# RWKV products by head, a compact state updated by VectorE, and the order of work around the triangular inverse

## The chip, the core and the metric

The kernel runs on one NeuronCore of a Trainium2 chip. TensorE (PE) multiplies matrices, its weight loads (PEld) running beside the products; VectorE (DVE), ScalarE (ACT) and GpSimd (POOL) work on tiles; SyncE (SP) issues most transfers. The metric is the device time of one execution in microseconds (us). Lower is better.

## The reference, cut to what matters

Two layers run over 256 context tokens and 1024 image tokens. In each a projection feeds four mixers (RWKV-7, S5, SSD, GLA), whose outputs are joined and projected back. The change touches the RWKV mixer alone: four heads, two directions, a 64x64 state S for each.

```python
def rwkv7_scan(r, w, k, v, kk, a, s0, reverse, need_out):
    def step(S, inp):
        r_t, w_t, k_t, v_t, kk_t, a_t = inp
        sa = jnp.einsum('bhvk,bhk->bhv', S, -kk_t)
        S = S * w_t[:, :, None, :] + sa[..., None] * (kk_t * a_t)[:, :, None, :] + v_t[..., None] * k_t[:, :, None, :]
        y = jnp.einsum('bhvk,bhk->bhv', S, r_t) if need_out else None
        return S, y
```

## The kernel before, in words

A layer has three stages: the projection with the GLA and SSD mixers in its shadow, the RWKV stage with the S5 mixer in its shadow, and the output projection.

The RWKV stage, `rw`, walks ten windows of 128 tokens, both directions at once. A window has two chunks `s` of 64 tokens. The index `u`, 0 to 3, is direction times two plus head pair. A head pair fills 128 partitions, head `h` in its 64-partition half. Five steps stand one iteration apart, so that iteration `i` holds step `st` of window `i - st`:

- `rw_elem` (0): decays and scaled keys: `AR` (the operands that meet the state), `BK`, the chunk decay `PM`, the bonus sum `ks`.
- `rw_pair` (1): the products of `BK` and `AR` within a chunk, masked into `A`. As both heads lie under one another, `AR` is first copied by POOL into a zeroed tile `r_AD` that keeps the heads apart. `BK`, scaled and transposed, becomes `Bt`; 32x32 diagonal blocks of `A` are copied to `r_Ad` by ACT.
- `rw_inv` and `rw_vals` (2): the inverse of the triangular matrix, `TT`. VectorE transposes `r_Ad` into `r_N`, then does fifteen dependent pairs `r_tp`, `r_X`, then transposes and four small products.
- `rw_chain` (3): the only serial work between windows, twice per window: products with `UV` and `S` into `X`, a copy to `rs`, the product with `TT`, a copy into `UV`, the product with `Bt`, the new `S`. The outputs gather in the same bank as `X` and leave it as `yw`.
- `rw_out` and `rw_final` (4): outputs are moved out of `yw` by products with the constant `IJ`, summed over directions in `r_yt`, normed and gated.

The state `S`, `rs` and `TT` hold both heads on the diagonal of a zeroed [128, 4, 128] (or [128, 8, 64]) tile. A product with a bf16 zero tile `r_z` opens each `X` bank.

The Tile framework draws dependences and waits. A list scheduler sets each engine's order: among what is ready by its own model it takes what was traced first. `ORDER = (3, 2, 4, 1, 0)` is the order of tracing within an iteration; S5 quarters, `gelu` and `gate` (`side`, at iterations `SJ`) are traced ahead of it. Each engine then runs its own list strictly in order.

Of the kernel before, what the change touches and what calls it, by code (L numbers as in the profile page):

```python
# [15 lines left out]
OP = mybir.AluOpType  # L16
# [71 lines left out]
CON, ACON, RCON = {}, {}, {}  # L88
for _d, _l in ((CON, [("ident", 128), ("ones", 128), ("bones", 128), ("eps", 1), ("gneps", 1), ("one", 1)]),
               (ACON, [("triF", 128), ("triB", 128), ("gmF", 64), ("gmB", 64), ("bm4", 4), ("c16", 16), ("reset64", 256)]),  # L90
               (RCON, [("IJ", 128), ("vinit", 256), ("rm", 128), ("m16", 32), ("reset64", 256)])):
    _o = 0
    for _n, _c in _l:
        _d[_n] = (_o, _c)
        _o += _c
# [6 lines left out]
def constants():  # L102
# [24 lines left out]
    ij = np.zeros((128, 128))  # L127
    ij[64:, :64] = np.eye(64)
    ij[:64, 64:] = np.eye(64)[::-1]
    put("IJ", ij)  # L130
# [108 lines left out]
RA = "pvpv"  # L239
AA = "ppvv"  # L240

EG = dict(bk="aa", ad="pppp", dg="aaaa", bb="pp", b0="p", b1="v", tk="pp", am="p", ar="vp", sp="p", bt="aa")

RN = (3, 2, 10)
NF = 2
# [9 lines left out]
class K:  # L255
# [864 lines left out]
    def rw(self, outs, side={}):  # L1120

        nc, c = self.nc, self.c
        self.rz = {}
        for p, ns in (("re", "in th a cs eP BK AD Ad N X Am tp Rm Bb"), ("rx", "AR A"), ("rl", "ks yt fin f0 yw")):
# [9 lines left out]
        self.zero = self.S("r_z", [128, 512], mybir.dt.bfloat16)  # L1134
        nc.gpsimd.memset(self.zero, 0.0)
        self.rsc = dict(okb=okb, kah=kah, w0=w0h, a0=a0h)
        self.ks, self.yt = {}, {}
        S = None
        Ws = [dict(w=w, bi=[w, 1 - w if w < 2 else 11 - w], need=outs or w >= 2) for w in range(10)]
        for i in range(10 + 4):  # L1140
            for f in side.get(i, ()):
                f()
            for st in ORDER:
                k = i - st
                if not 0 <= k < 10:
                    continue
                W = Ws[k]
                if st == 0:
                    self.rw_elem(W)
                elif st == 1:  # L1150
                    self.rw_pair(W)
                elif st == 2:
                    self.rw_inv(W)
                    self.rw_vals(W)
                elif st == 3:
                    S = self.rw_chain(W, S)
                else:
                    self.rw_out(W)
                    if W["need"] and not self.rw_first(W, 0):
                        self.rw_final(W["bi"])  # L1160

    def rw_first(self, W, d):

# [67 lines left out]
    def rw_pair(self, W):  # L1231
# [5 lines left out]
        for d in range(2):  # L1237
            z = self.rzero("r_AD", [128, 2, 2, 2, 2, 64], 1)
            for h in range(2):
                q = slice(64 * h, 64 * h + 64)  # L1240
                self.copy(EG["ad"][2 * d + h], z[q, :, :, h, :n // 64], AR[q, d, :, :, :n // 64])
            for s in range(2):
                ps = self.P("pb")
                for hp in range(2):
                    self.mm(ps[:, hp * 256:(hp + 1) * 256], BK[:, d * 2 + hp, s].rearrange("p k t -> p (k t)"),
                            z[:, hp, s].rearrange("p h k t -> p (h k t)"))
                self.tt(A[:, s, 2 * d:2 * d + 2].rearrange("p u h f -> p (u h) f"), ps.rearrange("p (a f) -> p a f", a=4),
                        c("rm").unsqueeze(1).to_broadcast([128, 4, 128]), OP.mult)
# [21 lines left out]
    def rw_inv(self, W):  # L1270
# [11 lines left out]
        for i in range(15, 0, -1):  # L1282
            r0 = i // 4
            sh = [128, 2, i, 4 - r0]
            self.tt(tmp[:, :, :i, r0:], N[:, :, i, 0:i].unsqueeze(3).to_broadcast(sh), X[:, :, i:i + 1, r0:4].to_broadcast(sh), OP.mult)
            self.tt(X[:, :, :i, r0:4], X[:, :, :i, r0:4], tmp[:, :, :i, r0:], OP.add)
# [61 lines left out]
    def rw_chain(self, W, S):  # L1348
        nc = self.nc
        A, AR, Bt, TT, UV, PM = [W[n] for n in ("A", "AR", "Bt", "TT", "UV", "PM")]  # L1350
        w, need = W["w"], W["need"]
        if need:
            yw = W["yw"] = self.R("r_yw", [128, 2, 256], 1)
        hs = [slice(64 * h, 64 * h + 64) for h in range(2)]
        for s in range(2):
            last = w == 9 and s == 1
            X = self.P("px").rearrange("p (u f) -> p u f", u=4)
            self.mm(X.rearrange("p u f -> p (u f)"), self.zero[:, 0:128], self.zero, True, False)
            for u in range(4):
                for h in range(2):  # L1360
                    self.mm(X[0:64, u, hs[h]], A[:, s, u, h, 0:64], UV[:, s, u, hs[h]], False, False)
            if S is not None:
                for u in range(4):
                    ar = AR[:, u // 2, u % 2, s]
                    if need:
                        self.mm(X[:, u], ar.rearrange("p k t -> p (k t)"), S[:, u], False, False)
                    else:
                        self.mm(X[0:64, u], ar[:, 0], S[:, u], False, u == 3)
            rs = self.rzero("r_rs", [128, 4, 128], 2)
            nc.vector.tensor_copy(rs[0:64, :, 0:64], X[0:64, :, 0:64])  # L1370
            nc.scalar.copy(rs[64:128, :, 64:128], X[0:64, :, 64:128])  # L1371
            ps = self.P("pu")[0:64].rearrange("p (u v) -> p u v", u=4)
            for u in range(4):
                self.mm(ps[:, u], TT[:, s * 4 + u], rs[:, u])
            nc.vector.tensor_copy(UV[0:64, s, 0:2], ps[:, 0:2])  # L1375
            nc.scalar.copy(UV[0:64, s, 2:4], ps[:, 2:4])
            Sn = None
            if not last:
                X2 = self.P("pu").rearrange("p (u f) -> p u f", u=4)
                for u in range(4):  # L1380
                    self.mm(X2[:, u], Bt[:, s, u], UV[:, s, u])

                Sn = self.rzero("r_S", [128, 4, 128], 2)
                for h in hs:
                    if S is None:
                        nc.vector.tensor_copy(Sn[h, :, h], X2[h, :, h])
                    else:
                        self.tt(Sn[h, :, h], S[h, :, h], PM[h, s].unsqueeze(2).to_broadcast([64, 4, 64]), OP.mult, EG["sp"])
                        self.tt(Sn[h, :, h], X2[h, :, h], Sn[h, :, h], OP.add)
            if need:  # L1390
                for u in range(4):
                    for h in range(2):
                        self.mm(X[64:128, u, hs[h]], A[:, s, u, h, 64:128], UV[:, s, u, hs[h]], False, u == 3 and h == 1)
                for d in range(2):
                    o = yw[64:128, s] if d == 0 else yw[0:64, s]
                    nc.scalar.copy(o, X[64:128, 2 * d:2 * d + 2].rearrange("p u f -> p (u f)"))
            S = Sn
        return S

    def rw_out(self, W):  # L1400

        nc, c, bi = self.nc, self.c, W["bi"]
        if not W["need"]:
            return
        b, first, yw = min(bi), self.rw_first(W, 0), W["yw"]
        ps = self.P().rearrange("p (s a d t) -> p s a d t", s=2, a=2, d=2)
        for s in range(2):
            for hp in range(2):
                self.mm(ps[:, s, hp].rearrange("p d t -> p (d t)"), yw[:, s, hp * 128:(hp + 1) * 128], c("IJ"))
        if first:  # L1410
            self.yt[b] = self.R("r_yt", [128, 2, 2, 128], 4)
        for d in range(2):
            o = self.yt[b][:, int(bi[d] != b)].rearrange("p a (s t) -> p a s t", t=64)
            v = ps[:, :, :, d].rearrange("p s a t -> p a s t")
            if d:
                o = o[:, :, ::-1]
            if first:
                nc.scalar.copy(o, v)
            else:
# [396 lines left out]
```

## Time and profile before

| | |
|---|---|
| median of three runs | 2279.06 us (2275.93 to 2290.05) |
| the profiled execution | 2286.73 us, of it 2284.7 us from the first to the last instruction |
| PE, PEld, DVE, ACT, POOL busy | 86%, 72%, 69%, 41%, 37% |
| RWKV stage, first layer | 664 to 1058 us |
| RWKV stage, second layer | 1730 to 2140 us |

Busy shares are means over stages of different limits, so the stages have to be read apart. A PE that is busy by the page can have pipelined products whose ends are modelled. The stage borders are set by eye: the loads of the first window and of the output weights.

### The profile page before, as it was taken

How to read it: one execution, taken by the hardware profiler on the slowest of the kernel's cores; microseconds unless marked ns; L12 is line 12 of the kernel's file. 1: busy time of each engine (PE TensorE's matmuls, PEld its weight loads, DVE VectorE, ACT ScalarE, POOL GpSimd, SP SyncE). 2: the span in 40 equal slices, each digit the busy share in tenths (PEclk: the TensorE clock that was granted, in tenths of full speed). 3: DMA queues.
4: the chain of work that ended last, by engine and by line, in shares of the span. 5: the costliest groups of instructions: out<-in, count | busy, mean ns of one | idle time of the engine just before them, and what ended most of it. 6: DMA issues, size and time to landing. Idle time of an engine off the chain costs nothing.

```text
span 2284.7 us, 44162 instructions
## 1 busy us (share of the span) xinstructions
PE 1958.3 (86%) x17176; PEld 1645.4 (72%) x17176; DVE 1574.8 (69%) x3513; ACT 926.8 (41%) x2006; POOL 835.5 (37%) x947
## 2 busy tenths in 40 slices
PE   7797999999986887788998989989995567879897
PEld 5677787777764766677997777867884556767797
DVE  3876535857539888876577877377563998787654
ACT  3345212244435565553323552113442554655420
POOL 1446431203345436333222456301233554443322
PEclk9899999999997899899998989989997777989998
DMA  8134314454343223213333354134223322220432
GB/s 273 50 117 163 131 52 123 141 182 123 116 144 103 86 87 119 68 45 118 102 106 110 119 170 143 59 97 139 70 70 96 127 84 80 69 65 30 146 104 93
DMA packets 208049, 246.76 MB, mean 108 GB/s; under 512 B 28384, under 2 KB 150240, under 8 KB 207840
## 3 DMA queue, kind: packets, MB, share of 16 engines
q1 hardware_dynamic: 174832, 215.49, 30.1%
q10 hardware_dynamic: 33008, 28.45, 3.8%
q8 instruction: 135, 2.21, 0.4%
q14 instruction: 74, 0.61, 0.1%
HBM read 169.27 MB, written 76.71 MB: 108 GB/s over the span
## 4 chain that ended last, share of the span: by engine, by line
PE 31%; DVE 23%; ACT 5%; issue 4%; DMA 4%; POOL 3%; SPq 1%; DVEq 0%; ACTq 0%; POOLq 0%
PE pj L320 18%; PE ps L320 3%; DVE r_X L332 2%; DVE r_tp L332 2%; PE pu L320 2%; PE px L320 2%; PE pb L320 2%; PE p L320 1%; DMA o_w<-in_wout 1%; DVE r_N L1275 1%; PE pc L320 1%; DVE r_A L332 1%; DMA o_y<-yd 1%; DVE z_x L332 1%; DVE r_BK L332 1%
## 5 line engine op out<-in xcount | busy, mean ns | idle before, releaser
L320 PE MATMUL pj<-hi,i_wh 128*128 128x512 f32 (+1 forms) x952 | 249.6, 382 | 22.9 <-DVE hi L1524 10.9
L320 PE MATMUL pj<-hi,i_wl 128*128 128x512 f32 (+1 forms) x952 | 247.2, 373 | 0.0
L320 PE MATMUL pj<-lo,i_wh 128*128 128x512 f32 (+1 forms) x952 | 246.6, 375 | 0.0
L320 PEld LDWEIGHTS pj<-hi,i_wh 128*128 128x128 f32 x952 | 170.3, 197 | 58.2 <-DVE hi L1524 11.3
L320 PEld LDWEIGHTS pj<-lo,i_wh 128*128 128x128 f32 x952 | 170.7, 196 | 34.7 <-issue 4.4
L320 PEld LDWEIGHTS pj<-hi,i_wl 128*128 128x128 f32 x952 | 166.4, 192 | 34.1 <-issue 5.0
L320 PE MATMUL pb<-r_AD,r_BK 128*128 128x256 f32 x320 | 104.0, 479 | 49.9 <-DVE r_BK L332 34.0
L332 DVE TENSOR_TENSOR i_wl<-i_w,i_wh 128x512 fp32r<-128x512 f32 x108 | 87.6, 818 | 73.3 <-ACT i_wh L1547 36.5
L1547 ACT CAST i_wh<-i_w 128x512 fp32r<-128x512 f32 x108 | 66.3, 619 | 163.3 <-PE pj L320 126.5
L320 PEld LDWEIGHTS pb<-r_AD,r_BK 128*128 128x128 f32 x320 | 73.1, 241 | 66.5 <-issue 22.8
L320 PE MATMUL px<-r_UV,r_A 128*64 128x64 f32 x1216 | 100.9, 237 | 11.4 <-DVE r_UV L1375 8.7
L320 PEld LDWEIGHTS px<-r_UV,r_A 128*64 128x64 f32 x1216 | 86.1, 147 | 32.2 <-DVE r_UV L1375 10.6
L332 DVE TENSOR_TENSOR r_X<-r_X,r_tp 128x30 f32<-128x30 f32 (+1 forms) x300 | 92.1, 307 | 6.5
L332 DVE TENSOR_TENSOR r_tp<-r_N,r_X 128x30 f32<-128x30 f32 (+1 forms) x300 | 88.1, 294 | 6.4
L332 DVE TENSOR_TENSOR g_Y<-pc,g_Y 64x256 f32<-64x256 f32 x70 | 29.4, 422 | 75.8 <-ACT g_Y L535 54.9
L320 PE MATMUL pj<-i_wh,hi 128*128 128x256 f32 x448 | 71.9, 298 | 9.4 <-ACT i_o L329 5.1
L335 POOL TENSOR_SCALAR r_AD<-r_AR 64x512 f32<-64x512 f32 (+1 forms) x80 | 56.1, 702 | 64.8 <-PE pb L320 43.1
L320 PE MATMUL pu<-r_rs,r_TT 128*64 128x128 f32 x320 | 52.5, 317 | 29.9 <-ACT r_rs L1371 29.8
L329 ACT ACTIVATE r_BK<-r_BK,r_PM 128x128 f32<-128x128 f32 x160 | 59.8, 399 | 31.4 <-PE pb L320 30.0
L320 PEld LDWEIGHTS pj<-i_wh,hi 128*128 128x128 f32 x448 | 62.1, 199 | 13.7 <-ACT i_o L329 5.5
L320 PEld LDWEIGHTS pu<-r_rs,r_TT 128*64 128x64 f32 x320 | 41.7, 160 | 39.4 <-ACT r_rs L1371 34.4
L332 POOL TENSOR_TENSOR s_Y<-s_Y,s_yt 128x256 f32<-128x256 f32 x34 | 29.2, 870 | 111.0 <-DVE s_Y L332 62.2
(466 smaller groups left out, 5166.4 us busy)
## 6 DMA issues: line engine op xcount, KB each, us to landing
i_w<-in_win SPq DMA_DIRECT2D x108, 256.0 KB, 3.0
r_in<-rm SPq DMA_DIRECT2D x36, 512.0 KB, 4.2
a_w<-in_ada SPq DMA_DIRECT2D x64, 256.0 KB, 3.1
rm<-i_o SPq DMA_DIRECT2D x48, 256.0 KB, 2.7
o_y<-yd SPq DMA_DIRECT2D x36, 256.0 KB, 3.1
i_o<-in_ada SPq DMA_DIRECT2D x32, 256.0 KB, 4.7
z_st<-s5t SPq DMA_DIRECT2D x32, 256.0 KB, 3.0
o_w<-in_wout SPq DMA_DIRECT2D x32, 256.0 KB, 3.2
```

Source lines behind the costliest of these rows:

```text
L320: self.nc.tensor.matmul(out, lhsT, rhs, start=start, stop=stop, skip_group_check=True)
L329: self.nc.scalar.activation(out=out, in_=in_, func=f, **kw)
L332: (self.nc.vector if e == "v" else self.nc.gpsimd).tensor_tensor(out, a, b, op)
L335: (self.nc.vector if e == "v" else self.nc.gpsimd).tensor_scalar(out, a, s1, s2, op0, op1)
L1275: nc.vector.transpose(Nt[:, :1024].rearrange("p (i j) -> p i j", j=32), AD.rearrange("p u t -> p t u").unsqueeze(2).to_broadcast([128, 32, ...
L1547: self.nc.scalar.copy(hi[:, v], w)
```

## The change

- Each head's product is a product of its own that reads and writes that head's half of the partitions: twice as many products of half the width. The zeroed copies (`r_AD`), the zero product, the constant `IJ` and the diagonal form of `S` and `rs` go. `S` is [128, 4, 64], one head in either half.
- The new state is made by four `scalar_tensor_tensor` instructions on VectorE. Before, POOL multiplied and VectorE added.
- `rs` is copied by one VectorE instruction for both heads. `UV` has two buffers instead of one.
- The outputs are made in `rw_out`, which `rw_chain` now calls: per chunk and `u` two products with the state and two with `A`, straight into the layout that `yw` and `IJ` gave.
- `issue_after` puts each VectorE instruction that an iteration traces after the inverse (final, pair, elem and side work) behind that inverse's last `r_X` in VectorE's order. The side work is traced last.

```diff
         for i in range(10 + 4):
-            for f in side.get(i, ()):
-                f()
...
+            with ExitStack() as es:
+                for st in ORDER:
...
+                            self.rw_inv(W)
+                            self.rw_vals(W)
+
+                            es.enter_context(self.tc.issue_after(W["last"]))
...
+                for f in side.get(i, ()):
+                    f()
@@ rw_pair
-            z = self.rzero("r_AD", [128, 2, 2, 2, 2, 64], 1)
-                self.copy(EG["ad"][2 * d + h], z[q, :, :, h, :n // 64], AR[q, d, :, :, :n // 64])
...
+        for s in range(2):
+
+            ps = [self.P("pb").rearrange("p (u f) -> p u f", u=4) for _ in hs]
+            for u in range(4):
+                for h in range(2):
+                    self.mm(ps[h][:, u, :n], BK[hs[h], u, s].rearrange("p k t -> p (k t)"),
+                            AR[hs[h], u // 2, u % 2, s, :n // 64].rearrange("p k t -> p (k t)"))
             for h in range(2):
+                self.tt(A[:, s, :, h, :n], ps[h][:, :, :n], c("rm")[:, :n].unsqueeze(1).to_broadcast([128, 4, n]), OP.mult)
@@ rw_vals
-        UV = self.rzero("r_UV", [128, 2, 4, 128], 1)
+        UV = self.R("r_UV", [128, 2, 4, 128], 2)
@@ rw_chain
+            X = self.P("px")[:, :256].rearrange("p (u v) -> p u v", u=4)
+            for u, h in uh:
+                self.mm(X[hs[h], u], A[:, s, u, h, 0:64], UV[:, s, u, hs[h]], u == 0, S is None and u == 3)
+            if S is not None:
+                for u, h in uh:
+                    self.mm(X[hs[h], u], AR[hs[h], u // 2, u % 2, s, 0], S[hs[h], u], False, u == 3)
+            rs = self.R("r_rs", [128, 4, 64], 2)
+            nc.vector.tensor_copy(rs, X)
+            ps = self.P("pu")[:, :256].rearrange("p (u v) -> p u v", u=4)
+            for u, h in uh:
+                self.mm(ps[hs[h], u], TT[hs[h], s * 4 + u], rs[hs[h], u])
+            nc.vector.tensor_copy(UV[0:64, s, :, hs[0]], ps[hs[0]])
+            nc.scalar.copy(UV[0:64, s, :, hs[1]], ps[hs[1]])
...
+                for u, h in uh:
+                    self.mm(X2[hs[h], u], Bt[:, s, u, hs[h]], UV[:, s, u, hs[h]])
...
+                    for u in range(4):
+                        self.stt(Sn[:, u], S[:, u], PM[:, s, u:u + 1], X2[:, u], OP.mult, OP.add)
...
+            self.rw_out(W, at)
@@ rw_out
+        for s, S in enumerate(at):
             for u in range(4):
...
+                    for h in hs:
+                        self.mm(o[h], S[h, u], AR[h, u // 2, u % 2, s, 1], True, False)
+                for i, h in enumerate(hs):
+                    self.mm(o[h], UV[:, s, u, h], A[:, s, u, i, 64:128], S is None, True)
```

What moves is best seen in the built order. VectorE before, in the first layer, inside the inverse of the seventh window (`r_tp`, `r_X`; names with `z_` are S5 work, `r_DT` and `pi` are the window before):

```order
L332 TENSOR_TENSOR r_X<-r_X,r_tp 128x2x15
L332 TENSOR_TENSOR z_b_9514<-z_b_9514,z_st 128x640
L332 TENSOR_TENSOR z_t_9531<-z_t_9531,z_t_9532 128x640
L332 TENSOR_TENSOR r_tp<-r_N,r_X 128x2x14
L332 TENSOR_TENSOR z_b_9514<-z_b_9514,z_b_9499 128x640
L988 SCALAR_TENSOR_TENSOR z_t_9531<-z_st,z_t_9531 128x640
L332 TENSOR_TENSOR r_X<-r_X,r_tp 128x2x14
L988 SCALAR_TENSOR_TENSOR z_b_9514<-z_st,z_b_9514 128x640
L332 TENSOR_TENSOR r_DT<-r_DT,pi 128x256
L332 TENSOR_TENSOR z_a<-z_t_9531,z_st 128x640
L332 TENSOR_TENSOR r_tp<-r_N,r_X 128x2x13
```

Between the dependent pairs of the inverse stand seven other instructions, six of them S5 work of 640 columns, and each delays the next pair by its own length.

VectorE in the changed kernel, where the sixth inverse ends and the seventh begins:

```order
L1278 TENSOR_TENSOR r_X<-r_X,r_tp 128x2x4
L967 COPY z_b_9210<-p_9211 64x480
L1281 STREAM_TRANSPOSE r_DT<-r_X 128x256
L1283 STREAM_TRANSPOSE r_DN<-r_DT 128x256
L328 TENSOR_TENSOR r_A<-pb,rcon 128x4x128 x2
L1362 COPY r_UV<-pu 64x4x64
L334 SCALAR_TENSOR_TENSOR r_S<-r_S,r_PM,pu 128x64 x4
L328 TENSOR_TENSOR r_A<-pb,rcon 128x4x128 x2
L967 COPY z_b_9210<-p_9218 64x160
L1267 STREAM_TRANSPOSE r_N<-r_Ad 128x1024
L328 TENSOR_TENSOR r_tp<-r_N,r_X 128x2x15
L1278 TENSOR_TENSOR r_X<-r_X,r_tp 128x2x15
```

The S5 work has left the inverse, the pair's masks `r_A` stand in twos behind it, and the next inverse's transpose follows the last mask with one small copy between.

TensorE before, one chunk of the chain and the output products of the window before (`r_yw`):

```order
L320 MATMUL px<-r_z 128x512
L320 MATMUL px<-r_UV_6857,r_A 64x64 x8
L320 MATMUL px<-r_S_7098,r_AR 128x128 x4
L320 MATMUL px<-r_UV_6857,r_A 64x64 x8
L320 MATMUL ps<-r_in,rconm 128x128 x4
L320 MATMUL pu<-r_rs_7079,r_TT_6808 64x128 x4
L320 MATMUL ps<-rcon,r_yw 128x128 x4
L320 MATMUL px<-r_UV_6857,r_A 64x64 x4
```

Two groups of sixteen narrow instructions, with the constant `IJ` and the products for outputs between them, surround four wide products.

TensorE in the changed kernel, one chunk of the chain:

```order
L316 MATMUL px<-r_S,r_AR 64x64 x8
L316 MATMUL px<-r_UV,r_A 64x64 x8
L316 MATMUL pu<-r_rs,r_TT_6807 64x64 x8
L316 MATMUL ps<-r_A,r_UV 64x64
L316 MATMUL pu<-r_UV,r_Bt 64x64 x8
L316 MATMUL ps<-r_A,r_UV 64x64
L316 MATMUL ps<-r_AR,r_S 64x64 x2
L316 MATMUL ps<-r_A,r_UV 64x64 x2
L316 MATMUL ps<-r_AR,r_S 64x64 x2
```

The zero product is gone, each group of four wide products is a group of eight narrow ones, and the outputs come in twos behind the chain's products, changing between products with the state (64 partitions deep) and with `A` (128 deep). The order lists a float product once; the trace shows it as two instructions.

## Rows read from the trace of the kernel before

**Rows 1.** The page: span, and busy time of each engine

```profile
span 2284.7 us, 44162 instructions
PE 1958.3 (86%) x17176; PEld 1645.4 (72%) x17176; DVE 1574.8 (69%) x3513; ACT 926.8 (41%) x2006; POOL 835.5 (37%) x947
```

**Rows 2.** Busy time by window, the two RWKV stages; columns as the first row names them

```profile
core 0: us, PE busy (x) PEld busy (x) DVE busy (x) ACT busy (x) POOL busy (x), PEclk, DMA share, GB/s
...
664.00:1058.00 394.00, 308.56 (x3686) 256.82 (x3684) 325.38 (x737) 215.30 (x510) 179.51 (x250) 0.87 0.30 92
...
1730.00:2140.00 410.00, 301.21 (x3653) 252.23 (x3652) 328.40 (x717) 209.31 (x498) 187.58 (x252) 0.83 0.25 79
```

**Rows 3.** The same view, first layer, from one inverse's start to the next

```profile
913.00:949.00 36.00, 28.94 (x334) 24.46 (x333) 35.14 (x69) 18.36 (x44) 20.25 (x29) 0.79 0.21 59
...
987.50:1025.00 37.50, 32.64 (x431) 26.65 (x434) 29.08 (x72) 21.40 (x50) 16.27 (x23) 0.91 0.05 16
1025.00:1058.00 33.00, 30.65 (x451) 25.33 (x439) 24.49 (x81) 12.09 (x26) 8.12 (x10) 0.90 0.15 40
```

**Rows 4.** Groups by line and tile, whole span: busy, mean ns, idle before

```profile
L320 PE MATMUL pb<-r_AD,r_BK 128*128 128x256 f32 x320 | 104.0, 479 | 49.9 <-DVE r_BK L332 34.0
L332 DVE TENSOR_TENSOR r_X<-r_X,r_tp 128x30 f32<-128x30 f32 (+1 forms) x300 | 92.1, 307 | 6.5
L332 DVE TENSOR_TENSOR r_tp<-r_N,r_X 128x30 f32<-128x30 f32 (+1 forms) x300 | 88.1, 294 | 6.4
L335 POOL TENSOR_SCALAR r_AD<-r_AR 64x512 f32<-64x512 f32 (+1 forms) x80 | 56.1, 702 | 64.8 <-PE pb L320 43.1
L332 POOL TENSOR_TENSOR r_S<-r_S,r_PM 64x256 f32<-64x256 f32 x72 | 50.5, 701 | 33.7 <-DVE r_S L332 28.0 <-DVE r_S L1386 2.5
L332 DVE TENSOR_TENSOR r_S<-pu,r_S 64x256 f32<-64x256 f32 x72 | 30.1, 418 | 21.3 <-PE pu L320 18.9 <-POOL r_f L332 1.3
L1375 DVE COPY r_UV<-pu 64x256 f32<-64x256 f32 x40 | 16.4, 410 | 17.8 <-PE pu L320 17.6
L1370 DVE COPY r_rs<-px 64x256 f32<-64x256 f32 x40 | 16.3, 408 | 10.4 <-PE px L320 9.7
L1371 ACT COPY r_rs<-px 64x256 f32<-64x256 f32 x40 | 14.6, 364 | 69.5 <-DVE r_rs L1370 60.6 <-DVE r_X L332 8.6
L332 DVE TENSOR_TENSOR r_A<-pb,rcon 128x512 f32<-128x512 f32 x80 | 54.1, 683 | 19.5 <-PE pb L320 19.2
L1275 DVE STREAM_TRANSPOSE r_N<-r_Ad 128x1024 f32<-128x1024 f32 x20 | 39.4, 1969 | 7.6 <-ACT r_Ad L1040 7.3
L1040 ACT COPY r_Ad<-r_A 32x256 f32<-32x256 f32 x80 | 32.2, 402 | 8.6 <-DVE r_A L332 7.5 <-POOL r_AD L335 0.3
L332 DVE TENSOR_TENSOR r_BK<-r_th,r_cs 128x512 f32<-128x512 f32 x20 | 25.8, 1288 | 4.8 <-POOL r_th L332 3.5 <-POOL r_eP L1196 1.3
```

**Rows 5.** VectorE's timeline, first layer: start, us, engine, line, operation

```profile
907.54 0.68 DVE L332 TENSOR_TENSOR r_BK<-r_th,r_cs 128x512 f32<-128x512 f32 x1
...
909.02 1.25 DVE L332 TENSOR_TENSOR r_tp<-r_N,r_X 128x24 f32<-128x24 f32 x1
```

**Rows 6.** Tile `r_tp`, one inverse: ns min/median/max, first and last start, forms

```profile
L332 DVE TENSOR_TENSOR r_tp<-r_N,r_X x15: 166/195/616, 830.2 to 848.2; 128x24 f32<-128x24 f32 x3, 128x30 f32<-128x30 f32 x2, 128x36 f32<-128x36 f32 x2, 128x28 f32<-128x28 f32 x1
```

**Rows 7.** TensorE's timeline, three places: rows times columns used, moving size, count

```profile
837.59 1.09 PE L320 MATMUL ps<-con,qfy 128*64 128x128 f32 x16
838.52 0.63 PE L320 MATMUL px<-r_UV,r_A 128*64 128x64 f32 x8
...
919.77 0.75 PE L320 MATMUL pi<-r_DN,r_Am 32*32 32x32 f32 x64
...
941.35 1.15 PE L320 MATMUL px<-r_UV,r_A 128*64 128x64 f32 x16
942.43 1.16 PE L320 MATMUL px<-r_S,r_AR 128*128 128x128 f32 x8
943.52 1.15 PE L320 MATMUL px<-r_UV,r_A 128*64 128x64 f32 x16
```

More of the change, by code (lines that the diff above doesn't have):

```diff
@@ L1123, in rw @@
         self.rz = {}
[L1124 removed]
+        for p, ns in (("re", "in th a cs eP BK Ad N X Am tp Rm Bb"), ("rx", "AR A"), ("rl", "ks yt fin f0")):
             self.where.update({"r_" + n: p for n in ns.split()})
@@ L1140, in rw @@
         for i in range(10 + 4):
-            for f in side.get(i, ()):
-                f()
[L1143 to L1160, printed above, removed]
+            with ExitStack() as es:
+                for st in ORDER:
+                    k = i - st
+                    if 0 <= k < 10:
+                        W = Ws[k]
+                        if st == 0:
+                            self.rw_elem(W)
+                        elif st == 1:
+                            self.rw_pair(W)
+                        elif st == 2:
+                            self.rw_inv(W)
+                            self.rw_vals(W)
+                            es.enter_context(self.tc.issue_after(W["last"]))
+                        elif st == 3:
+                            S = self.rw_chain(W, S)
+                        elif W["need"] and not self.rw_first(W, 0):
+                            self.rw_final(W["bi"])
+                for f in side.get(i, ()):
+                    f()
     def rw_first(self, W, d):
@@ L1285, in rw_inv @@
             self.tt(tmp[:, :, :i, r0:], N[:, :, i, 0:i].unsqueeze(3).to_broadcast(sh), X[:, :, i:i + 1, r0:4].to_broadcast(sh), OP.mult)
-            self.tt(X[:, :, :i, r0:4], X[:, :, :i, r0:4], tmp[:, :, :i, r0:], OP.add)
+            last = nc.vector.tensor_tensor(X[:, :, :i, r0:4], X[:, :, :i, r0:4], tmp[:, :, :i, r0:], OP.add)
+        W.update(last=last.ins)
         DT = self.R("r_DT", [128, 32, 8], 2)
@@ L1351, in rw_chain @@
         w, need = W["w"], W["need"]
-        if need:
-            yw = W["yw"] = self.R("r_yw", [128, 2, 256], 1)
+        hs = [slice(64 * h, 64 * h + 64) for h in range(2)]
+        uh = [(u, h) for u in range(4) for h in range(2)]
+        at = []
+        for s in range(2):
+            at.append(S)
+            X = self.P("px")[:, :256].rearrange("p (u v) -> p u v", u=4)
[11 more added lines that the diff above has]
+            nc.scalar.copy(UV[0:64, s, :, hs[1]], ps[hs[1]])
+            Sn = None
+            if not (w == 9 and s == 1):
+                X2 = self.P("pu")[:, :256].rearrange("p (u v) -> p u v", u=4)
+                for u, h in uh:
+                    self.mm(X2[hs[h], u], Bt[:, s, u, hs[h]], UV[:, s, u, hs[h]])
+                Sn = self.R("r_S", [128, 4, 64], 3)
+                if S is None:
+                    nc.vector.tensor_copy(Sn, X2)
+                else:
+                    for u in range(4):
+                        self.stt(Sn[:, u], S[:, u], PM[:, s, u:u + 1], X2[:, u], OP.mult, OP.add)
+            S = Sn
@@ L1354, in rw_chain, with rw_out @@
+        if need:
+            self.rw_out(W, at)
+        return S
+    def rw_out(self, W, at):
+        nc, bi = self.nc, W["bi"]
+        A, AR, UV = [W[n] for n in ("A", "AR", "UV")]
+        b, first = min(bi), self.rw_first(W, 0)
         hs = [slice(64 * h, 64 * h + 64) for h in range(2)]
[L1355 to L1358, printed above, removed]
+        ps = self.P().rearrange("p (s a d t) -> p s a d t", s=2, a=2, d=2)
+        for s, S in enumerate(at):
@@ L1359, in rw_chain @@
             for u in range(4):
[L1360 to L1409, printed above, removed]
+                o = ps[:, s, u % 2, u // 2]
```

23 lines of the change are left out of this document (5 added, 18 removed).

## Prediction

> **What bounds the kernel now.** I read the page's totals first, then the stages by window, then the windows of the stage, then the groups behind each wait. The whole-span shares mislead here: PE is busy for 86% and DVE for 69% [rows 1], but the change lies in the two RWKV stages, where VectorE is busy for 325.4 of 394 us and 328.4 of 410, TensorE for 308.6 and 301.2 [rows 2]. Cut by inverse, the middle of the first stage is VectorE's alone (35.1 of 36.0 us), and the idle time sits at its ends: 8.4 us between the ninth and tenth inverse, 8.5 us after the tenth [rows 3]. All of VectorE's idle time in both stages is 394 − 325.4 + 410 − 328.4 = 150.2 us. So three kinds of gain are possible: VectorE's instructions get shorter (middle), its waits get shorter (ends), or work moves from the full iterations into the idle ones. What shortens TensorE or ScalarE alone in the middle is worth nothing.
>
> **The change part by part.** All sums are over both layers and stand against the profiled execution of 2286.7 us, which is 7.7 above the median.
>
> *POOL's work that goes.* `r_AD` 56.1 us and the state's multiply 50.5 us, 106.6 together [rows 4], of 179.5 + 187.6 = 367.1 us of POOL in the stages [rows 2]. POOL itself bounds nothing, but VectorE's small instructions run longer beside it: the `r_tp` of 24 elements at 909.02 took 1.25 us [rows 5], where the middle one of an inverse takes 0.195 and the shortest 0.166 [rows 6]. `r_X` and `r_tp` take 180.2 us in 600 instructions [rows 4]; at 0.195 each it would be 117, so 63 us are stretch. If all of it comes from POOL evenly, each POOL us costs 0.17, and 106.6 of them 18. `r_BK` shows the same: mean 1.288 [rows 4] against 0.68 in its short case [rows 5], 20 × 0.61 × 106.6/367.1 = 3.5. VectorE's other instructions have no such pair of rows; I add 3 for them. Taken −25. Bounds: 0 (the stretch comes from POOL's other instructions, which fill the room) and −45 (twice the even share).
>
> *The new state on VectorE.* 72 additions at 0.418 (30.1 us) go [rows 4]; 144 `scalar_tensor_tensor` of 64 columns on 128 partitions come. The trace has none of that shape. Nearest are `r_tp` (at most 36 columns, 0.195) [rows 6] and `r_A` (512 columns, 0.683) [rows 4]: a line between them gives 0.23 at 64 columns, 144 × 0.23 = 33 us, +3. Bounds: at the shortest `r_tp`, 0.166, −6; at the mean `r_tp`, 0.294, +12. Taken +4, near the line. The `rs` copy on 128 partitions has as many columns as the one it replaces (40 × 0.408): 0. `r_A` stays at 80 instructions, eight of them halved: 0.
>
> *The chain's step.* A step is products into `px`, `rs`, product with `TT`, `UV`, product with `Bt`, `S`. Today three groups of eight full-width instructions of 128 columns lie on it; one takes 943.52 − 942.43 = 1.09 us start to start [rows 7]. Sixteen instructions on alternate halves of the partitions, 128 columns each, started and were done in 838.52 − 837.59 = 0.93 [rows 7]: two run at once. With 64 columns a group is then about 0.5, so three of them save 1.8, less some 0.1 each where the form changes. ScalarE's half of `rs` starts only after VectorE's (60.6 us of waiting for it in 40) and takes 0.364 [rows 4]: gone. The state's four instructions instead of one add 0.1 to 0.5. A step gets shorter by some 1.8 us, 72 over 40 steps. But most of it is hidden: VectorE, which has other work queued between, waits behind the chain for only 18.9 (`r_S`), 17.6 (`r_UV`) and 9.7 (`r_rs`), 46.2 us in all [rows 4]. I take under half of that, −20, since what VectorE does in the meantime is not free to start earlier. Bounds 0 and −46.
>
> The Trainium skill bears on this one: its page "TensorEngine Tiling (Array Packing)", section Restrictions and Gotchas, says that different row tiles cannot access the same PSUM bank simultaneously, and here both heads' products write one bank. The trace speaks against it as a rule on time: 64 products of 32x32, `pi`, which by the code take four groups of 32 partitions in turn and write one bank, are through in 0.75 us [rows 7], 12 ns each. It is a rival below.
>
> *The pair behind the inverse.* The masks `r_A` and the next `r_N` now stand at one place of VectorE's order, with the whole inverse behind them. Masks wait for products: today 19.2 us [rows 4]. The products themselves get cheaper: `pb` takes 104.0 us now [rows 4] and about half on alternate halves, two banks together after sixteen instructions (some 0.9), where one today takes four (104.0 × 4/320 = 1.3). After the second pair of masks two copies `r_Ad` on ScalarE (0.402 each [rows 4]) and their hand-overs must end before `r_N`: about 1.1 us × 20 = 22, where today 7.3 are waited [rows 4]: +15 with the products even. What hides it is one S5 copy in the order shown. Bounds: −10 (cheaper products take half of the 19.2) and +60 (3 us a window more).
>
> *Side work last.* S5's quarters leave the middle of the inverse. The total of VectorE's work stays, so a full iteration gains nothing; but the last quarter can now fall behind the ninth inverse, where VectorE idles 8.4 us [rows 3]. Twice that, less what of the work already fits, −14. Bounds −17 and +15 (it ends so late that S5's output is waited for).
>
> *The drain.* After the tenth inverse two steps, outputs and the last norm follow one another, with VectorE idle 8.5 us [rows 3]. Two steps per layer shorter by 1.8 are −7; the `yw` copies and `IJ` products on the way out go too, −2. Taken −9, bounds 0 and −12.
>
> Gone without a price: `r_z`, the constant, the memsets, ACT's `rs` and `yw` copies; TensorE's and ScalarE's room in the middle is idle already.
>
> Sum: −25 + 4 − 20 + 15 − 14 − 9 = **−49**. 2286.7 − 49 = 2237.7 profiled, less 7.7: median **2230**.
>
> **Rivals.**
> *Serial path through the pair (slower).* The chain, side work and pair are no longer spread over the inverse, so products, masks, ScalarE's copies and `r_N` become one path on which VectorE stands: per window 0.9 for the products behind whatever chain products TensorE has queued (up to 2), 1.2 for the first mask pair's wait, 1.1 for the copies, some 5.5 us × 20 = 112. The other terms give −64, so it decides from 64 us on, 3.2 us a window above today's (19.2 + 7.3)/20 = 1.3. All of it: −64 + 112 = +48, 2327. For it: the order shows one copy between the last mask and `r_N`. Against: `r_rs`, `r_S` and final work of the older window are ready at that time. Chance 0.12.
> *Nothing to speak of.* POOL's other work moves into the freed room and stretches as much; the chain's time was hidden; the pair eats the drain's gain: −10, 2269. For it: VectorE's own instructions get no fewer (3513 of them [rows 1] become some 70 more). Chance 0.17.
> *The idle time halves.* With TensorE's part of pair and chain halved and VectorE's order free of foreign work, half of the 150.2 goes, −75; with POOL's −25 and the state's +4, −96: 2183. For it: TensorE is busy 32.6 of 37.5 and 30.7 of 33 us in the last windows [rows 3], so there its relief counts twice. Chance 0.16.
> *Two heads in one bank take turns.* Then `px`, `TT` and `Bt` groups cost 1.09 like today's sixteen narrow ones (942.43 − 941.35 [rows 7]); a step gains 0.3 instead of 1.8, the chain term falls to −3, the drain to −2: −25, 2254. By the Trainium skill's rule on banks, cited above, this is what would happen. Chance 0.05.
>
> **How the numbers follow.** The forecast of 2230 has 0.50. A measurement of this kernel can tell about 1%, 23 us, from no change. Faster by more: forecast 0.47 of its 0.50, the halved idle time 0.16, the turns 0.02, 0.04 from the weak end of "nothing": 0.69. Slower by more: the serial path, 0.11. The rest, 0.20, is within 1%. The range leaves out the serial path and the far end of the halving: 2178 to 2285.
>
> **What the profile after would show.** POOL's busy time falls by 100 us and the mean `r_tp` from 0.294 towards 0.25: the first term; if POOL falls and `r_tp` doesn't, the term is wrong. 144 `r_S` near 0.23. Eight 64x64 products of a chain group (sixteen rows) within 0.5 us: the chain's step; at 1.1 the turns. Idle before `r_S`, `r_UV`, `r_rs` down from 46.2 to some 26. Idle before `r_A` and `r_N` together near 40; over 90 would mean the serial path. VectorE's idle share behind the ninth inverse near nothing. The stages some 25 us shorter each; a change elsewhere than in them would make all of this wrong, as would the S5 output appearing late at the third stage.

## The result, and the profile after

The changed kernel takes 2351.97 us (2347.48 to 2356.78), the kernel before 2282.42 in the same comparison: ratio 1.0312 [1.0291, 1.0334], slower by 70 us where 50 less were forecast. The profiled execution took 2347.48 us, 61 more than that of before.

The page of the changed kernel, first lines, answers to [rows 1]:

```profile
span 2345.7 us, 47086 instructions
PE 1963.9 (84%) x18800; PEld 1636.5 (70%) x18800; DVE 1554.7 (66%) x3583; ACT 882.3 (38%) x1893; POOL 724.0 (31%) x781
```

Every engine but TensorE is busy for less than before (VectorE by 20 us, POOL by 111), and the span is longer. So the loss is waiting. For the place I cut the two RWKV stages from their first `r_th` to their last `r_yt`, the end of the norm. Windows of the kernel before, cut so:

```profile
core 0: us, PE busy (x) PEld busy (x) DVE busy (x) ACT busy (x) POOL busy (x), PEclk, DMA share, GB/s
671.00:1110.00 439.00, 349.62 (x4097) 294.62 (x4096) 344.95 (x774) 232.41 (x544) 197.23 (x262) 0.88 0.31 96
1739.00:2193.00 454.00, 338.35 (x3964) 286.12 (x3964) 356.18 (x777) 227.22 (x531) 202.81 (x262) 0.84 0.27 86
```

The same view of the changed kernel:

```profile
669.00:1145.00 476.00, 352.81 (x4900) 288.12 (x4898) 333.63 (x810) 207.19 (x480) 142.52 (x181) 0.73 0.29 88
1776.00:2271.00 495.00, 359.15 (x4913) 299.59 (x4911) 350.05 (x837) 207.00 (x481) 150.15 (x184) 0.72 0.26 81
```

The stages are 78 us longer together (971 for 893), the rest is 17 shorter. In the stages VectorE is busy 17 us less and idle 95 us more, 287 for 192. TensorE is busy 712 us instead of 688, at a granted clock of 0.73 and 0.72 for 0.88 and 0.84: it works for longer, and more of the time at the lower of its two levels (1.2 and 2.4 GHz).

Groups of VectorE of the changed kernel, which answer to [rows 4]:

```profile
L1278 DVE TENSOR_TENSOR r_X<-r_X,r_tp 128x30 f32<-128x30 f32 (+1 forms) x300 | 84.6, 282 | 7.6
L328 DVE TENSOR_TENSOR r_tp<-r_N,r_X 128x30 f32<-128x30 f32 (+1 forms) x300 | 75.4, 251 | 7.8
L328 DVE TENSOR_TENSOR r_A<-pb,rcon 128x512 f32<-128x512 f32 (+1 forms) x80 | 50.0, 655 | 36.5 <-PE pb L316 36.2
L1267 DVE STREAM_TRANSPOSE r_N<-r_Ad 128x1024 f32<-128x1024 f32 x20 | 39.4, 1970 | 23.0 <-ACT r_Ad L1036 22.9
L334 DVE SCALAR_TENSOR_TENSOR r_S<-r_S,r_PM,pu 128x64 f32<-128x64 f32 x144 | 30.7, 273 | 29.0 <-PE pu L316 29.0
L328 DVE TENSOR_TENSOR r_BK<-r_th,r_cs 128x512 f32<-128x512 f32 x20 | 18.6, 930 | 2.6 <-POOL r_th L328 2.6
L1358 DVE COPY r_rs<-px 128x256 f32<-128x256 f32 x40 | 16.5, 414 | 17.8 <-PE px L316 17.7
L1362 DVE COPY r_UV<-pu 64x256 f32<-64x256 f32 x40 | 16.4, 410 | 20.1 <-PE pu L316 19.9
```

The last column holds the surprise: waits behind the chain rose from 46.2 to 29.0 + 17.7 + 19.9 = 66.6 us where 26 were forecast, those of the pair from 26.5 to 59.1 where some 41 were. The busy column went as forecast.

TensorE's two groups of output products in the changed kernel:

```profile
L316 PE MATMUL ps<-r_A,r_UV 128*64 128x64 f32 x576 | 68.7, 285 | 17.9 <-DVE r_UV L1362 17.8
...
L316 PE MATMUL ps<-r_AR,r_S 64*64 64x64 f32 x560 | 55.9, 283 | 15.7 <-ACT r_a L325 13.4 <-DVE r_S L334 1.7 <-DVE r_yt L334 0.5
```

They take 124.6 us, in 1136 instructions. And TensorE's timeline there (start, us; each row a run of one form):

```profile
863.13 0.34 PE L316 MATMUL ps<-r_A,r_UV 128*64 128x64 f32 x4
863.40 0.33 PE L316 MATMUL ps<-r_AR,r_S 64*64 64x64 f32 x4
863.66 0.34 PE L316 MATMUL ps<-r_A,r_UV 128*64 128x64 f32 x4
863.92 0.33 PE L316 MATMUL ps<-r_AR,r_S 64*64 64x64 f32 x4
```

Four instructions of one form take 0.26 us until the next form starts. This is what the experiments turn out to be about.

### The profile page after: what moved, and what is told of

Same layout as the page of the kernel before. It is cut to its first block, busy times and chain, and to the rows that moved or that the text cites. A ratio compares the mean times of both kernels' runs of the same rounds, so it can differ in the third digit from the quotient of the medians.

```text
span 2345.7 us, 47086 instructions
## 1 busy us (share of the span) xinstructions
PE 1963.9 (84%) x18800; PEld 1636.5 (70%) x18800; DVE 1554.7 (66%) x3583; ACT 882.3 (38%) x1893; POOL 724.0 (31%) x781
## 4 chain that ended last, share of the span: by engine, by line
PE 51%; DVE 26%; DMA 8%; ACT 6%; issue 5%; POOL 2%; SPq 1%; ACTq 0%; DVEq 0%; POOLq 0%
PE pj L316 31%; PE ps L316 8%; PE pc L316 2%; DVE r_X L1278 2%; PE p L316 2%; DVE r_tp L328 2%; DVE z L328 2%; PE pb L316 2%; DMA o_w<-in_wout 1%; PE pi L316 1%; DMA o_y<-yd 1%; PE pu L316 1%; PE pz L316 1%; DVE r_N L1267 1%; DVE r_cs L1188 1%
## 5 line engine op out<-in xcount | busy, mean ns | idle before, releaser
L316 PE MATMUL pb<-r_AR,r_BK 64*128 64x128 f32 (+1 forms) x640 | 86.4, 383 | 33.5 <-POOL r_BK L328 13.0
L316 PEld LDWEIGHTS pb<-r_AR,r_BK 64*128 64x128 f32 x640 | 72.4, 271 | 41.0 <-POOL r_BK L328 23.2
L1278 DVE TENSOR_TENSOR r_X<-r_X,r_tp 128x30 f32<-128x30 f32 (+1 forms) x300 | 84.6, 282 | 7.6
L331 POOL TENSOR_SCALAR r_Bb<-r_A 32x256 f32<-32x256 f32 x40 | 17.0, 425 | 227.5 <-DVE r_A L328 219.8
L316 PE MATMUL ps<-r_A,r_UV 128*64 128x64 f32 x576 | 68.7, 285 | 17.9 <-DVE r_UV L1362 17.8
L328 DVE TENSOR_TENSOR r_tp<-r_N,r_X 128x30 f32<-128x30 f32 (+1 forms) x300 | 75.4, 251 | 7.8
L316 PE MATMUL ps<-r_in,rconm 128*128 128x128 f32 x320 | 60.0, 344 | 20.9 <-ACT r_a L325 14.3
L328 DVE TENSOR_TENSOR r_A<-pb,rcon 128x512 f32<-128x512 f32 (+1 forms) x80 | 50.0, 655 | 36.5 <-PE pb L316 36.2
L316 PEld LDWEIGHTS ps<-r_in,rconm 128*128 128x128 f32 x320 | 52.5, 246 | 26.5 <-ACT r_a L325 16.9
L1307 ACT COPY r_TT<-r_DT 32x256 f32<-32x256 f32 x80 | 52.3, 654 | 46.2 <-DVE r_DT L328 45.4
```

What stands on the lines that cost most here:

```text
L316: self.nc.tensor.matmul(out, lhsT, rhs, start=start, stop=stop, skip_group_check=True)
L328: (self.nc.vector if e == "v" else self.nc.gpsimd).tensor_tensor(out, a, b, op)
L331: (self.nc.vector if e == "v" else self.nc.gpsimd).tensor_scalar(out, a, s1, s2, op0, op1)
L1278: last = nc.vector.tensor_tensor(X[:, :, :i, r0:4], X[:, :, :i, r0:4], tmp[:, :, :i, r0:], OP.add)
L1307: nc.scalar.copy(TT[q, :, 32 * b:32 * b + 32], DT[q].rearrange("p c u -> p u c"))
```

## The experiments

Kernels measured together shared a chip and the runs of the kernel before, whose median moved between 2280.8 and 2284.7 from one group of kernels to the next; a difference between kernels of two groups is uncertain by some 4 us for that reason alone.

**The order, undone and alone.** Two rival theories of the loss stood first: the narrow products (they leave TensorE at its lower level), or the order (the pair queued behind the inverse). Run e1 takes both parts of the order from the changed kernel:

```diff
             with ExitStack() as es:
+                for f in side.get(i, ()):
+                    f()
...
-                            es.enter_context(self.tc.issue_after(W["last"]))
...
-                for f in side.get(i, ()):
-                    f()
```

> The changed kernel with the order of before: side work traced first, nothing queued behind the inverse; products, state and outputs by head stay. Clock theory (the narrow products leave TensorE at its lower level for more of the RWKV stage, whatever the order): granted clock of the two stages stays near the changed kernel's 0.73 and 0.70, time 2325 to 2360. Order theory (the pair queued behind the inverse makes VectorE wait, and TensorE's idle time then lowers its clock): clock back to 0.83 or more, the waits before r_A and r_N back to some 27 us, time 2230 to 2290.

Run e2 puts the same order on the kernel before; run e3 removes only `issue_after` from the changed kernel.

> The kernel before with the order of the change alone: final, pair, elem and side work of an iteration behind the inverse's last r_X on VectorE, side work traced last. Clock theory: the products are as wide as before, so the clock stays at 0.83 or more; the waits before r_A and r_N grow from 27 to some 55 us, and the time is within 25 us of before's. Order theory: clock near 0.75, time 2330 to 2360, as the change.

> The changed kernel without the queueing behind the inverse, but with the side work still traced last: it tells the two parts of the order apart. If the queueing is what costs, this runs like the run with the whole order undone; if the place of the side work is what costs, like the changed kernel, 2352. Clock theory: within 15 us of the changed kernel.

| | order of before | side work last | and queued behind the inverse |
|---|---|---|---|
| wide products | 2284.7 | | 2269.4, ratio 0.9941 [0.9919, 0.9963] |
| products by head | 2330.9, 1.0211 [1.0187, 1.0235] | 2350.9, 1.0297 [1.0273, 1.0322] | 2352.0, 1.0312 [1.0291, 1.0334] |

The lower row holds everything of the change but the order, the compact state with it. It costs 46 us under the old order and 83 under the new; the order gains 15 with the wide ones and loses 21 with the narrow ones. So the order theory fell as the main cause, and the place of the side work, not the queueing, is what cost with narrow products. In e2 the waits before `r_A` and `r_N` rose from 26.5 to 34.0 us, less than was expected. The clock stayed at 0.73 and 0.72 in e1, as the clock theory has it; whether it is the cause was open.

**Lifting the clock.** e4 adds 32 filling products per iteration to the changed kernel, f3 adds 12 to e1, g4 the same 12 in 64 by 64:

```diff
+                if 1 <= i <= 12:
+                    F = self.P("px")
+                    for _ in range(12):
+                        self.mm(F, self.fz[:, 0:128], self.fz)
```

> The changed kernel plus 32 products of a bf16 zero tile (128x128 by 128x512, into a px bank that nobody reads) in each of twelve iterations, traced last, so that they fill what the scheduler takes for TensorE's idle time: 768 over both layers, some 165 us of TensorE at the higher level. They compute nothing. Clock theory: granted clock of the stages rises to 0.9 or more, r_in's products fall from 344 to some 300 ns, and in spite of the added work the time falls by 30 us or more, below 2320. Order theory: the waits before r_A and r_N stay near 59 us, the time is that of the change or up to 40 us more.

> The run with the order undone plus 12 filling products of a zero tile in each of twelve iterations (288 in all, some 62 us of TensorE at the higher level), a lighter dose than the 32 before; they compute nothing. Clock theory: the stages' clock rises from 0.73 to some 0.8 and the time falls to 2300 to 2325. If the lower clock only goes along with the waits and is not what makes them: 2330 to 2345.

> As the run with 12 filling products (2305, clock 0.80 and 0.81), but each filling product uses 64 partitions and 64 columns of weights instead of 128 and 128, with the same 512 columns moving: the same number, about the same time on TensorE. If the width of the products counts for the granted clock: clock stays near 0.74 and the time at 2325 to 2345. If only TensorE's being busy counts: clock 0.80 and 2300 to 2312.

e4: clock 0.84 and 0.83, and 2372.7 us, 1.0398 [1.0365, 1.0431], some 20 slower than without. f3: 2305.0, 1.0108 [1.0083, 1.0133], 26 faster than e1. g4: clock 0.76 and 0.76, 2364.6, 1.0352 [1.0303, 1.0402], 34 slower than e1. Stage windows of f3:

```profile
675.00:1126.00 451.00, 354.96 (x5006) 276.74 (x5006) 326.24 (x806) 207.22 (x479) 142.97 (x179) 0.80 0.29 91
1755.00:2220.00 465.00, 353.99 (x4996) 276.88 (x4995) 339.88 (x827) 208.39 (x481) 146.71 (x181) 0.81 0.27 84
```

A higher clock went with a gain once (f3) and with a loss twice (e4, g4). Two more runs test its rank: 12 fills on e2's wide kernel (g3), and on a kernel with the cure below (g1).

> The kernel before with the order of the change (2269) plus the 12 filling products. If the lower clock (0.85 and 0.84 there) costs in the wide kernel too: stages' clock 0.9 or more and 2245 to 2262. If only the narrow products leave a clock that is worth lifting: 2265 to 2285.

> The run with the order undone, with both cures: output products in two groups per chunk (alone 2331 to 2296) and 12 filling products of a zero tile per iteration (alone 2331 to 2305). If the changes of form and the lower clock are two causes: the gains add, 2265 to 2280, stages' clock at 0.8. If both work by the same route (TensorE's queue comes free sooner): 2290 to 2300.

g3: clock 0.90 and 0.88, 2296.4 us, 27 slower than e2. g1: 0.81 and 0.80, 2299.1, 1.0072 [1.0048, 1.0096], no better than its base f2 (2296.1). The clock can be lifted, but with the outputs cured it brings nothing, as was expected for the case that both work by one route. That the time the fills take on TensorE's queue eats the gain is argued, not shown. What speaks most against the clock as the main cause are two runs without fills, g2 and h2 below.

**The pair.** f1 puts the wide pair (`r_AD` by POOL, one bank at a time) back into e1; f4 gives `pb` three banks and `px` one in e1.

> The run with the order undone, and in it the pair as before: POOL copies AR into r_AD, four full-width products fill one bank, two banks in flight. Chain, state and outputs by head stay. If the pair by head is what costs (two banks filled together, so products and masks of a half take turns; half-deep products), the time comes down from 2331 to 2300 or less, the waits before r_A from 31 to some 20 us and before r_N from 17 to some 8. If the chain and the outputs are what costs, it stays within 10 us of 2331. If the clock is what costs, and the pair's full-width products lift it, the granted clock of the stages rises from 0.73 to 0.8 and the time falls by half of the way to before, to 2305.

> The run with the order undone, with three pb banks and one px bank instead of two and two. If the pair's two banks, filled together, are what holds VectorE's masks: waits before r_A fall from 31 to 20 us or less and the time by 10 to 25 us. If not: within 10 us of 2331, or slower where the chain's products wait for the one px bank.

f1: 2329.9 us, 1.0205 [1.0171, 1.0239]: nothing, though the stages' clock rose to 0.78 and 0.76. f4: 2358.1, 1.032 [1.0267, 1.0373], slower by 27, though its four executions lie apart (2335.8, the profiled one, and 2357.7 to 2362.2). In the profiled one the wait before `r_A` fell from 30.7 to 20.2 us, while that before `r_N` rose from 17.3 to 24.0. So the pair by head is not the cause, and a bank taken from the chain for it is no cure; what a third bank is worth by itself no run tells.

**The outputs.** f2 orders the output products of a chunk in two groups of one form each, on e1; g2 does it on the changed kernel, order and all:

```diff
-            for u in range(4):
-                o = ps[:, s, u % 2, u // 2]
-                if S is not None:
-                    for h in hs:
-                        self.mm(o[h], S[h, u], AR[h, u // 2, u % 2, s, 1], True, False)
-                for i, h in enumerate(hs):
-                    self.mm(o[h], UV[:, s, u, h], A[:, s, u, i, 64:128], S is None, True)
+            o = [ps[:, s, u % 2, u // 2] for u in range(4)]
+            if S is not None:
+                for u in range(4):
+                    for h in hs:
+                        self.mm(o[u][h], S[h, u], AR[h, u // 2, u % 2, s, 1], s == 0 and u == 0, False)
+            for u in range(4):
+                for i, h in enumerate(hs):
+                    self.mm(o[u][h], UV[:, s, u, h], A[:, s, u, i, 64:128], s == 0 and u == 0 and S is None, s == 1 and u == 3)
```

> The run with the order undone, with the output products of a chunk in two groups, first the four heads' pairs with the state, then those with A, instead of eight changes between them. If the changes of form and the length of the outputs on TensorE's queue are what costs: down by 10 to 30 us from 2331, the busy time of the output products down from 125 by 20 us or more. If the pair or the clock is what costs: within 8 us of 2331.

> The changed kernel, order and all, with the output products in two groups. If the changes of form cost the same under either order: 2352 - 35 = 2317. If it was the alternating outputs, standing in the chain's way just where the pair's products are waited for, that turned the order from a gain of 15 into a loss of 21: 2296 or less, and the waits before r_A and r_N fall from 59 to some 45 us.

f2: 2296.1 us, 1.0074 [1.0046, 1.0102], 35 faster than e1. g2: 2291.3, 1.0042 [1.0027, 1.0057], 61 faster than the changed kernel. The edit also opens each bank with one start flag instead of one per product, and it lets the scheduler move other rows. TensorE's timeline of g2, its groups, and the windows of its stages:

```profile
850.32 0.68 PE L316 MATMUL ps<-r_AR,r_S 64*64 64x64 f32 x16
850.93 0.69 PE L316 MATMUL ps<-r_A,r_UV 128*64 128x64 f32 x16
851.54 0.68 PE L316 MATMUL ps<-r_AR,r_S 64*64 64x64 f32 x16
```

```profile
L316 PE MATMUL ps<-r_A,r_UV 128*64 128x64 f32 x576 | 41.5, 259 | 15.2 <-DVE r_UV L1362 14.8
...
L316 PE MATMUL ps<-r_AR,r_S 64*64 64x64 f32 x560 | 31.5, 250 | 7.3 <-ACT r_a L325 3.1 <-DVE r_yt L334 2.3 <-DVE r_S L334 1.7
```

```profile
669.00:1122.00 453.00, 334.60 (x4914) 278.67 (x4913) 327.20 (x811) 206.55 (x480) 146.09 (x181) 0.75 0.30 93
1752.00:2211.00 459.00, 320.67 (x4864) 270.26 (x4863) 339.71 (x832) 206.17 (x480) 148.97 (x182) 0.76 0.28 86
```

Sixteen instructions in one form take 0.61 us from their start to the start of the next form, and four take 0.26. Both hold one change of form, so twelve instructions more take 0.35, 0.03 each, and what is left of either is the change, 0.15 us. The same 1136 instructions are through in 73.0 us instead of 124.6. An estimate from these rows: 36 chunks (576 products with `A`, sixteen a chunk) lose six changes each, 32 us at 0.15 and 43 at the 0.20 that the lower level shows further down; the rest would come from more of the work standing at the higher level. The stages' clock in g2 is 0.75 and 0.76, hardly above the changed kernel's: the 61 us come without it. Most of the 59 us that the stages are shorter (912 for 971) is waiting of VectorE, 245 for 287 us; VectorE's work is 17 shorter as well. With the outputs grouped, the order costs nothing any more: g2 is no slower than f2.

Such an edit also moves other rows of the order, so h1 tries a dose, four groups per chunk (u 0 and 1, then 2 and 3).

> The changed kernel with the output products of a chunk in four groups, between the changed kernel's eight (2352) and the two (2291): state products of u = 0 and 1, their A products, then the same for u = 2 and 3. If the number of changes of form is the cause: a dose, some 2310, TensorE's busy time on the outputs near 94 us (125 at eight, 76 at two). If two groups won by another order of everything else that the scheduler happened upon: 2291 or 2352, and no dose.

2332.2 us, 1.0217 [1.0182, 1.0252], slower than the 2310 expected. Its rows on TensorE:

```profile
L316 PE MATMUL ps<-r_A,r_UV 128*64 128x64 f32 x576 | 53.9, 284 | 15.4 <-DVE r_UV L1362 15.3
L316 PE MATMUL ps<-r_AR,r_S 64*64 64x64 f32 x560 | 43.4, 283 | 21.1 <-ACT r_a L325 15.2 <-DVE r_yt L334 3.9 <-DVE r_S L334 1.7
...
1027.48 0.45 PE L316 MATMUL ps<-r_AR,r_S 64*64 64x64 f32 x8
1027.86 0.45 PE L316 MATMUL ps<-r_A,r_UV 128*64 128x64 f32 x8
```

The groups take 53.9 + 43.4 = 97.3 us. Eight instructions to the next form take 0.38, as 0.03 each and 0.15 for the change give. Eight, four, two groups: TensorE 124.6, 97.3, 73.0 us; time 2352, 2332, 2291. TensorE's part follows the dose (27 and 24 us less). The time follows it in direction only, 20 and then 41 us less: the second step gives more than TensorE's saving. What the freed queue and what the moved rows gave apart from that isn't told.

**What is left.** h2 traces the grouped outputs behind the other steps of the iteration; h3 puts the wide pair back into g2.

> The changed kernel with the outputs in two groups, and traced behind the iteration's other steps instead of at the chain's end, so that they stand behind the pair's products in TensorE's order. If their place on TensorE's queue ahead of the pair's and the chain's products still costs: 2270 to 2285. If not: within 8 us of 2291.

> The changed kernel with the outputs in two groups and the pair as before (r_AD by POOL, full-width products, one bank at a time). The waits before r_A and r_N are 51 us with the pair by head and the order of the change, 34 in the kernel before with that order. If the pair by head accounts for what is left over the wide kernel under the same order (2291 to 2269): 2270 to 2280 and waits near 35. If not, as with the order undone, where this moved nothing: within 10 us of 2291.

h2: 2282.8 us, 1.0002 [0.9987, 1.0017], like the kernel before; h3: 2300.4, 1.0086 [1.0053, 1.0119], so the pair by head is not what keeps g2 above e2. VectorE's waits in h2, and the windows of its stages:

```profile
L328 DVE TENSOR_TENSOR r_A<-pb,rcon 128x512 f32<-128x512 f32 (+1 forms) x80 | 50.0, 654 | 24.3 <-PE pb L316 24.1
L1269 DVE STREAM_TRANSPOSE r_N<-r_Ad 128x1024 f32<-128x1024 f32 x20 | 39.4, 1969 | 26.4 <-ACT r_Ad L1036 26.4
L334 DVE SCALAR_TENSOR_TENSOR r_S<-r_S,r_PM,pu 128x64 f32<-128x64 f32 x144 | 30.5, 273 | 12.3 <-PE pu L316 12.2
L1360 DVE COPY r_rs<-px 128x256 f32<-128x256 f32 x40 | 16.5, 413 | 9.7 <-PE px L316 9.6
L1364 DVE COPY r_UV<-pu 64x256 f32<-64x256 f32 x40 | 16.3, 407 | 8.4 <-PE pu L316 8.1
...
668.00:1105.00 437.00, 318.51 (x4806) 264.02 (x4804) 321.92 (x805) 200.33 (x470) 138.18 (x175) 0.73 0.29 92
1758.00:2196.00 438.00, 320.81 (x4817) 272.28 (x4817) 334.38 (x814) 206.13 (x479) 144.00 (x181) 0.74 0.29 89
```

The waits behind the chain are 29.9 us here, from 46.2 before and 66.6 after the change. They are no measure of the time: h3 has 30.4 (12.6 + 8.0 + 9.8) and is 18 us slower, e2 has 39.5 and is the fastest. h2 is as fast as the kernel before with its stages at a clock of 0.73 and 0.74, no higher than in the changed kernel, so the lower clock alone does not make the loss. Cut in this way its stages take 875 us, 18 less than before, but the stretch between them, 1105 to 1758, takes 653 where it was 629; why is open. The best version of all is e2, 2269.4, the old products in the new order.

## Why the prediction was wrong

*What bounds the kernel.* "TensorE's and ScalarE's room in the middle is idle already" and "What shortens TensorE or ScalarE alone in the middle is worth nothing" is the step that failed: I read from it that longer work on TensorE costs nothing either. VectorE was busy 35.1 of 36.0 us in one window [rows 3], but that was one of the fullest. Two others of the middle, in the same view of the kernel before:

```profile
827.00:889.00 62.00, 50.12 (x652) 44.09 (x651) 50.13 (x108) 35.28 (x88) 32.67 (x43) 0.92 0.25 71
...
949.00:987.50 38.50, 32.09 (x428) 24.09 (x428) 26.00 (x67) 23.15 (x47) 5.97 (x10) 0.91 0.32 98
```

VectorE is idle for 11.9 and 12.5 us in them, more than in either window at the end (8.4 and 8.5), and TensorE is busy for 81% and 83%. So VectorE was waiting in the middle already. The stages then lost 17 us of VectorE's work and gained 95 of its waiting.

*The outputs were not costed.* They stand in the sum only as "the `yw` copies and `IJ` products on the way out go too, −2". I allowed "some 0.1 each where the form changes" on the chain's step (0.15 measured) and didn't apply it to the outputs, which change eight times per chunk. Grouping them is worth 61 us under the order of the change (2352 to 2291) and 35 under the old one: the largest term, and missing. No other single edit takes back as much.

*POOL's work that goes (−25).* The size held. `r_tp` fell from 0.294 to 0.251, `r_X` from 0.307 to 0.282, `r_BK` from 1.288 to 0.930: 12.7 + 7.5 + 7.2 = 27.4 us of VectorE. The mechanism is borne out in part: with `r_AD` back on POOL the three groups take 20 us more (f1 against e1) and 26 more (h3 against g2). But at like POOL work `r_tp` and `r_X` together take 142 us in g2 and 165 in h1, so the order of things moves them as much, and part of the 27 may be luck. The time didn't follow: VectorE waited instead.

*The new state (+4).* 30.7 us for 30.1: +0.6. One instruction took 0.273, not 0.23; the four overlap.

*The chain's step (−20).* The groups went as forecast where the clock was high: sixteen instructions on alternate halves are 0.61 us apart from the next group, change of form included, as the outputs of g2 show above, so two heads in one bank do not take turns; that rival is refuted. At the lower level a group stays busy for 1.12 instead of 0.68. VectorE's waits rose by 20 us instead of falling by 20. The outputs stood between the chain's products: with them grouped the waits are 55.1 (g2), grouped and traced late 29.9 (h2), against the 26 forecast. But grouped and with the wide pair they are 30.4 as well (h3), so the place of the outputs is not the only thing that sets them. And where they came near the forecast, the time was that of the kernel before or worse, not 2230.

*The pair behind the inverse (+15).* Mis-sized: +33 on waits of 26.5. In h2 still +24. In the wide kernel the same order gives 22.1 + 11.9, +7.5 (e2). The serial path was the rival I gave for "slower", but it was to decide from 64 us above today's on, with idle time over 90 us as its mark where 59.1 were found, and undoing the queueing (e3) or the pair (f1, h3) wins nothing: right sign, wrong mechanism, so that rival's sign came out by luck. (Its parts add up to 5.2 us a window, 104 in all, rather than 5.5 and 112.)

*Side work last (−14).* It left the middle and overshot. VectorE's last S5 instruction but one of the first layer, in the changed kernel:

```profile
1080.80 0.69 DVE L334 SCALAR_TENSOR_TENSOR z_sg<-z_sg,z_yy 128x512 f32<-128x512 f32 x1
```

Before it started at 990.76. The idle time behind the ninth inverse is filled as forecast, but what follows the tenth now holds side work, and 25.7 us of waiting:

```profile
995.90:1034.50 38.60, 22.89 (x214) 18.96 (x213) 35.45 (x72) 14.09 (x37) 16.61 (x20) 0.63 0.12 37
1034.50:1102.00 67.50, 58.21 (x907) 40.38 (x906) 41.76 (x126) 22.75 (x39) 6.99 (x7) 0.85 0.30 90
```

This looks like the +15 end of the term's bounds, S5's output being waited for, and with products by head, side work last does cost 20 us (e1 to e3). But the same instruction in e3:

```profile
986.84 0.69 DVE L334 SCALAR_TENSOR_TENSOR z_sg<-z_sg,z_yy 128x512 f32<-128x512 f32 x1 [1.17 <-ACT z_sg L325]
```

So the lateness comes with the queueing, not with being traced last, and it is not what costs: e3 has none and loses 20 us, e2 has it (1059.14) and is the fastest. From the tenth inverse to the last `r_yt` of the first layer e3 takes 93 us and e1 94; e3 loses its time before, from the first inverse to the tenth (356 us for 346). Why side work last costs there is open.

*The drain (−9).* From the tenth inverse to the last `r_yt` it is 1034 to 1145, 111 us, where it was 1025 to 1110, 85: the opposite sign. VectorE is idle for 49 us of it where it was 34. The runs split it: 94 us in e1, without the order, and 102 in e2, with the order and the wide products, so both parts of the change lengthen it.

What stays open: what keeps g2 22 us above e2, which share of the dose is the moved order, what the lower clock costs by itself, and why the same 12 fills gain 26 us on e1 and nothing on f2.

## What to carry to other kernels

Splitting products by head halved a group's time here (0.61 us for 1.09) only in a run of sixteen instructions of one form, and the time went again where the form changed every four; order the products so that a form is left as seldom as possible, and count the changes as instructions with a price of their own. "TensorE is idle in this stage" is no licence to add to it: between an engine that is busy all the time and one in whose lists it must wait, ask what the longest run of foreign work ahead of each awaited product is. An order that helps one set of products (−15) may hurt another (+21), so a change of both needs each alone as a run.

## What was not expected of the hardware

A change between 64*64 and 128*64 products costs 0.15 us at the higher level: runs of four, eight and sixteen instructions start 0.26, 0.38 and 0.61 apart, 0.03 for each instruction and 0.15 over. At the lower one groups of four start 0.41 apart:

```profile
1012.16 0.48 PE L316 MATMUL ps<-r_AR,r_S 64*64 64x64 f32 x4
1012.57 0.48 PE L316 MATMUL ps<-r_A,r_UV 128*64 128x64 f32 x4
1012.98 0.48 PE L316 MATMUL ps<-r_AR,r_S 64*64 64x64 f32 x4
```

With runs of eight they start 0.62 apart (h1) and with sixteen 1.05 (g2), 0.05 for each instruction and 0.20 for the change.

The Trainium skill says on its page "TensorEngine Tiling (Array Packing)", section Tiling Modes, that changing the tiling mode drains TensorE; the trace agrees, in that a change takes time, and adds the price.

The granted clock: 288 filling products of full width raised the stages of e1 from 0.73 and 0.72 to 0.80 and 0.81; the same number with 64 partitions and 64 columns left 0.76 and 0.76 (g4). With products by head it was 0.73 and 0.72 instead of 0.88 and 0.84, TensorE being busy for 712 of 971 us instead of 688 of 893. And a higher clock was not worth having for itself: of the four kernels with full-width fills two got slower by 20 us or more, one stayed, one gained.
